# Tokens ordered by place in the chunk from the S5 inputs to the output projection of a hybrid S5 and FoX layer

## The chip, the cores and the metric

The kernel runs on one core of a Trainium2 chip. The metric is the device time of one execution in microseconds. A core has a matrix engine (PE in the profile), a vector engine (DVE), a scalar engine (ACT), a general engine (POOL) and a sync engine (SP), which here only issues DMAs. PE reads its operands from SBUF and writes into PSUM banks of 512 fp32 per partition; the other engines read those banks and empty them. [...]

## The reference, cut to what matters

A prompt of 2,048 tokens and a sample (decode) sequence of 64 tokens pass through one layer with 1,024 channels. Cut to its core:

```
shift, scale, gate = split(silu(c) @ w_ada + b_ada)
h    = rmsnorm(x) * (1 + scale) + shift
u, z_s, q, k, v, z_a, f_logit = split(h @ w_in)         # widths 512 x 6, then 8
y    = Re(C x_t) + D u,  x_t = abar * x_(t-1) + bbar u  # 32 groups of 16 channels, 64 complex states each
y    = gelu(y);  y = y * sigmoid(y @ w_glu + b_glu) * silu(z_s)
o    = softmax(q k^T / 8 + cumulative log-forget, causal) v * silu(z_a)   # 8 heads of 64
out  = x + gate * (concat(y, o) @ w_out)
return out, k, v, log-forget and last states, for prompt and sample
```

The decode sequence uses the same weights with given states and 512 cached keys and values per head.

## The kernel before, in words

The program is one Python builder. A list scheduler orders each engine's instructions ahead of time; in the last stage (the block `e.ordered()`) and on PE from the GLU on, the order is that of the code. All DMAs are issued by SP, one after another in SP's order, so a DMA whose data is late holds back those behind it. Products that need more than one fp32r pass are written as `mm3`: three matmuls with high and low halves (`whi`, `wlo`, and the two halves of `h`).

The stages follow each other: 

1. **Modulation and norm** (0 to about 144 us). `Ada` computes shift, scale and gate; `norm` loads x in tiles of 128 tokens, normalizes them and transposes them into `h` with channels on partitions. `h` has four groups g of 512 tokens; group 3 also holds the 64 decode tokens.
2. **In-projection and S5** (to about 750 us). `natural` makes u, k, v and q with tokens on PSUM partitions (`whi`, `wlo` stream as 256 columns, 24 matmuls per tile of 128 tokens; 264 columns where the eight forget logits ride along with u). `gates` makes the two z with channels on partitions, 512 tokens wide. u is done first; the other ten parts (k, k, v, v, q, q and four of z) are done for groups 2 and 3 and then again for 0 and 1, and beside each of them runs one of the 16 sets of the S5 (`s5_step`, two groups of 16 channels each). The S5 takes the sequence in 256 chunks of 8 tokens (and 8 decode chunks). Per set it needs u as a matrix `us` whose partitions are (token in the chunk, channel) and whose columns are the 264 chunks. Since `u_d` in DRAM is [token, channel], `load` fetches 128 chunks at a time with channels innermost (256-byte pieces) into `un`, DVE reorders a copy into `ug` (L920), PE transposes `ug`, and ACT copies PSUM into `us` (L943, L944). After the scan over the chunks (DVE, POOL and ACT), `outs` multiplies with `us` and `aa` (the scanned states) as stationary operands and the tables `tm` and `ca` as moving operands of 128 columns; 128 chunks land on the PSUM partitions, and the 8 decode chunks take matmuls of their own. ACT's gelu writes into `un`, and `ys_d` [token, channel] is stored from it.
3. **GLU** (750 to about 840 us). `Glu` reads `yn` from `ys_d` with tokens on partitions, PE transposes it (four per turn), ACT scales it into `y`, ACT and a second engine split it into `yh` and `yl`, and `mm` multiplies 256 tokens at a time with `wgh`, `wgl` into bank `glu`: nine token groups (one of them the 64 decode tokens) in two halves of the channels, 18 steps. POOL multiplies with z, the result goes to `ms_d` [channel, token]. Between the steps, the maxima for the attention's softmax run on PE and DVE.
4. **Attention** (840 to about 1,268 us). `Attn.run` goes through 20 tiles (four head pairs, five query tiles each). At a tile's end DVE multiplies the PSUM result by z, `sums` takes the reciprocal by Ln and Exp on ACT and multiplies on POOL, and the tile goes to `ma_d` [channel, token]. Meanwhile the generator `Out.weights` loads and splits w_out and combines operands for the last stage.
5. **Output projection** (to the end). `Out.run` multiplies `concat(ms, ma)` with w_out by Strassen's scheme in Winograd's form for seven pairs of 128-token tiles; pair 0 (`plain`) and the decode tokens are done directly. The products need the sums t1 to t4 of w_out's blocks (`operands`, done during parts 7 to 9 of the second half of stage 2, stored in DRAM, fetched again), and the loads `m` of `ms_d` and `ma_d` for the next pair.

In the profile, all matmuls bear the line of one helper (L144) and transposes that of another (L147), so groups are told apart by names.

## Time and profile before

| | us |
|---|---|
| runs | 1444.43, 1442.08, 1444.85 (median 1444.43) |
| the profiled execution | 1442.57, with a span of 1440.7 |
| PE busy | 1353.2 (94%) |
| DVE, ACT, POOL busy | 974.2 (68%), 593.1 (41%), 508.4 (35%) |
| TensorE clock granted, mean | 0.977 |
| DMA engines busy | 44.5% of 16 engines |

The span runs from the first to the last instruction; the profiled time has 1.9 us around it. A matmul group's "busy" adds up the durations of single matmuls that overlap in the engine's pipeline; what one costs is the distance between the starts of two that follow each other. An fp32 matmul leaves two records. "Idle before" names the wait that ended last in front of a group.

### The profile page before, as it was taken

Reading aid. Unit: us, or ns where it says so; the run is one execution under the profiler, and the core shown is the slowest. Engines: PE = TensorE matmul, PEld = TensorE weight load, DVE = VectorE, ACT = ScalarE, POOL = GpSimd, SP = SyncE. Lnnn points to the kernel's source line nnn. Section 1 sums busy time; section 2 is a strip of 40 time slices with the busy share of each in tenths; the row PEclk is TensorE's granted clock in tenths of the full one; section 3 lists DMA queues with packets and bytes.
Section 4 is the critical chain, followed back from the end, with each engine's and each line's share of the span. In section 5 each row is a group of like instructions: output and inputs, shape, how many; then the busy total and the mean of one; then the engine's idle time right before and its main releaser. Section 6 shows DMA issues by size and latency. Waiting matters only on the chain. (4 is left out here: it accounts for less than half of the span.)

```text
span 1440.7 us, 26308 instructions
## 1 busy us (share of the span) xinstructions
PE 1353.2 (94%) x9630; PEld 1065.7 (74%) x9630; DVE 974.2 (68%) x2455; ACT 593.1 (41%) x1252; POOL 508.4 (35%) x472
## 2 busy tenths in 40 slices
...
GB/s 339 282 288 158 124 65 87 98 83 92 112 96 149 280 75 142 65 116 140 218 331 294 176 146 128 40 54 132 41 76 52 75 60 81 133 235 217 161 161 88
DMA packets 210073, 205.01 MB, mean 142 GB/s; under 512 B 67575, under 2 KB 162515, under 8 KB 208920
## 3 DMA queue, kind: packets, MB, share of 16 engines
q1 hardware_dynamic: 209944, 203.33, 44.5%
...
## 5 line engine op out<-in xcount | busy, mean ns | idle before, releaser
L144 PE MATMUL low<-whi,h 128*128 128x256 f32 (+1 forms) x2112 | 406.1, 289 | 14.4 <-DVE ev L566 8.7
L144 PEld LDWEIGHTS low<-whi,h 128*128 128x128 f32 x2112 | 336.6, 192 | 24.8 <-issue 15.1
L144 PE MATMUL low<-wlo,h 128*128 128x256 f32 (+1 forms) x1088 | 307.5, 286 | 0.0
L1252 DVE CUSTOM_DVE_ANT_0 pb<-twin,cb 128x512 bf16<-128x512 f32 (+3 forms) x328 | 199.8, 609 | 68.4 <-PE twin L144 53.1
L144 PEld LDWEIGHTS low<-wlo,h 128*128 128x128 f32 x1088 | 209.0, 192 | 1.5 <-issue 1.2
L336 ACT ACTIVATE p<-twin 128x1024 f32<-128x1024 f32 (+3 forms) x180 | 149.4, 839 | 120.5 <-PE twin L144 113.5
L144 PE MATMUL low<-h,whi 128*128 128x512 f32 (+1 forms) x640 | 174.0, 357 | 0.0
L144 PE MATMUL bank<-p,vt 128*64 128x512 f32 (+3 forms) x704 | 143.5, 531 | 0.0
L144 PE MATMUL twin<-qs,ks 64*128 64x512 f32 (+3 forms) x1056 | 134.0, 359 | 0.0
L311 POOL TENSOR_TENSOR qss<-qss,mhalf 128x4 f32<-128x4 f32 (+1 forms) x68 | 77.2, 1136 | 139.9 <-DVE qss L310 117.3
L144 PEld LDWEIGHTS low<-h,whi 128*128 128x128 f32 x640 | 112.7, 188 | 17.7 <-issue 1.7
L305 DVE TENSOR_TENSOR wlo<-wst,whi 128x512 fp32r<-128x512 f32 (+1 forms) x96 | 67.3, 718 | 69.2 <-ACT whi L303 67.6
L144 PE MATMUL low<-h,wlo 128*128 128x512 f32 (+1 forms) x320 | 114.0, 356 | 0.0
L1329 DVE TENSOR_TENSOR acc<-acc,p 128x1024 f32<-128x1024 f32 (+4 forms) x90 | 87.8, 975 | 36.8 <-ACT p L336 35.1
L144 PEld LDWEIGHTS twin<-qs,ks 64*128 64x128 f32 x1056 | 94.8, 190 | 11.1
L144 PE MATMUL twin<-sm,kb 64*128 64x512 f32 (+3 forms) x360 | 78.0, 429 | 21.6 <-DVE pm L1252 12.5
L144 PEld LDWEIGHTS bank<-p,vt 128*64 128x64 f32 x704 | 45.4, 141 | 64.9 <-issue 56.8
L144 PEld LDWEIGHTS twin<-sm,kb 64*128 64x128 f32 x360 | 34.5, 187 | 63.8 <-DVE pm L1252 34.1
L303 ACT CAST whi<-wst 128x512 fp32r<-128x512 f32 (+1 forms) x96 | 57.2, 621 | 52.7 <-DMA wst<-in_w_in_dram 36.2
L195 POOL TENSOR_TENSOR x<-x,ot 128x512 f32<-128x512 f32 (+1 forms) x34 | 52.3, 1539 | 72.5 <-DVE ot L1633 66.1
L144 PE MATMUL twin<-ks,qs 64*128 64x512 f32 (+3 forms) x328 | 70.3, 432 | 4.0 <-ACT p L336 2.9
L1329 POOL TENSOR_TENSOR acc<-acc,p 128x1024 f32<-128x1024 f32 x22 | 52.4, 2383 | 42.9 <-ACT p L336 42.9
...
## 6 DMA issues: line engine op xcount, KB each, us to landing
...
```

The source lines that it names most:

```text
L144: return self.keep(self.pe.matmul(*a, **kw))
L195: PL.tensor_tensor(out, x, y, op=op)
L303: S.copy(hi, x)
L305: V.tensor_tensor(lo, x, hi, op=ALU.subtract)
L311: PL.tensor_tensor(out, out, bc(mhalf[:out.shape[0]], list(out.shape)), op=ALU.pow)
L336: i = S.activation(out, x, func, **kw)
L1252: V.tensor_tensor_reduce(b[:, :n], ps[:, h, :n], cb[:, h, :n], 1.0, NEG, ALU.add, ALU.max, accum_out=self.pm[:, t, h, pi:pi + 1])
L1329: (PL if j else V).tensor_tensor(y[:rows, :, c0:nq], x[:rows, :, c0:nq], p[:rows, :, :n], op=ALU.add)
```

## The change

The change keeps every tensor from u to the output projection's input in one order of tokens: by place t = 0 to 7 in the chunk, and inside a place by chunk (256 prompt chunks and 8 decode chunks, 264 in all).

- `u_d` and `ys_d` become [place, channel, chunk]; `z_d`, `ma_d`, `ms_d` become [channel, place, chunk]. A tile of 128 tokens is now half a place: `rows` picks every eighth row of x, y, k, v and q.
- `inputs` makes u with channels on partitions (256 or 320 tokens wide) instead of `natural`; the forget logits ride along with k, and `logf` moves from before `s5.setup` into the second half, behind part 1, with two switches of ACT's table; the log-forgets are written to DRAM and read back in token order.
- `load` is one DMA per group straight into `us`; the copy to `ug`, the transposes and ACT's copies go. `outs` has `tm` and `ca` stationary and streams `us` and `aa`, 264 columns, decode included; gelu writes `ys`, stored by one DMA per group.
- The GLU goes by place (8 places, two halves, 16 steps of 264 columns) and needs no transposes; its multiplication by z moves from POOL to DVE. 
- Attention's last multiplication on DVE reads PSUM with a stride and the one on POOL reads `w` with a stride of 8 elements.
- `operands` works on half blocks of 256 columns and is called in parts 4 to 8 of the second half. In the output projection, pair 0 is now place 0 and its ms half is multiplied first for all four blocks; its ma half and the load `m` of `ma_d` for pair 1 come right after the last attention tile; t4's eight fetches, which stood directly ahead of the next pair's loads `m` on SP, now follow pair 0's first half and stand behind that load; t3's last piece moves to the same place; the splits of w_out lag their loads by two.

Cut to its core ("..." marks what is left out):

```diff
-    u_d = dram.tile([NT, SW], F32, name="u_d")
+    u_d = dram.tile([TC, SW, CW], F32, name="u_d")
...
+    def rows(ap, i):
+        v = ap.rearrange("(c t) w -> t c w", t=TC)
+        return v[i // 2, P * (i % 2):P * (i % 2) + P] if i < 16 else v
...
-            nc.sync.dma_start(x[:r], e.x_p[t0:t0 + r] if s == 0 else e.x_s)
+            nc.sync.dma_start(x[:r], e.rows(e.x_s if s else e.x_p, i))
...
-                    nc.sync.dma_start(e.z_d[row:row + P, 512 * g + t0:512 * g + t0 + w], th[:, :w])
+                    nc.sync.dma_start(e.z_d[row:row + P, t:t + n, :NCH], th[:, :n * NCH].rearrange("p (t c) -> p t c", t=n))
...
+    def load(self, s):
+        us = self.us[s] = self.up.tile([P, GS, CW], F32, name="us", bufs=3)
+        for g in range(GS):
+            self.e.nc.sync.dma_start(us[:, g], self.group(self.e.u_d, GS * s + g))
...
-        for g in range(GS):
-            pt = self.pst.tile([P, 512], F32, tag="tr", name="tr")
-            for i in range(2):
-                PE.transpose(pt[:, P * i:P * i + P], ug[i][:, q0 + g], e.ident)
-            S.copy(us[:, g, :NCH], pt[:, :NCH])
-        S.copy(us[:, :, NCH:], self.ud[:, GS * s:GS * s + GS])
...
+        for g in range(GS):
+            py = self.ps.tile([P, CW], F32, tag="s5", name="sy")
+            PE.matmul(py, tm[:, g], us[:, g], start=True, stop=False)
+            PE.matmul(py, ca[:, g, 8:16].rearrange("p t q -> p (t q)"), aa[:, g], start=False, stop=True)
+            e.act(y[:, g], py, AF.Gelu_apprx_tanh)
+            nc.sync.dma_start(self.group(e.ys_d, GS * s + g), y[:, g])
...
+    def part(self, b):
+        if b < self.steps:
+            hl = self.yt[b] = [self.wk.tile([P, 2, CW], F32R, name="y" + i, bufs=4) for i in "hl"]
+            self.e.split(self.y[b], *hl)
...
-        e.V.scalar_tensor_tensor(xw, xw, 1.0, self.yt[b][0][:, :, :w], op0=ALU.add, op1=ALU.mult)
-        e.pmul(xw, xw, self.z[b][:, :, :w])
+        e.V.scalar_tensor_tensor(x, x, 1.0, self.y[b], op0=ALU.add, op1=ALU.mult)
+        e.V.scalar_tensor_tensor(x, x, 0.25, self.z[b], op0=ALU.mult, op1=ALU.mult)
...
-        e.pmul(w[:, :n], w[:, :n], tile.z[:, :n])
+        e.pmul(tile.z, w[:, :n].rearrange("p (c t) -> p t c", t=TC), tile.z)
...
+                if not half[0]:
+                    if part == 1:
+                        e.table("natural_log_exp_and_others", AF.Tanh, AF.Gelu_apprx_tanh)
+                        ip.logf(s5.ps)
+                        e.table("gelu_apprx_tanh_and_others", AF.Exp, AF.Ln, AF.Abs)
+                    for i in {4: (0,), 5: (1,), 6: (2, 3), 7: (4, 5), 8: (6, 7)}.get(part, ()):
+                        out.operands(*divmod(i, 2))
```

What this does to the order of the instructions shows at three places. The first is PE in an S5 set, among the matmuls of the in-projection (`bank` and `low` are PSUM banks). Before, transposes and the outputs of one bank:

```order
L147 MATMUL low_128<-ident_0_82,ug_192512_1_3165 128x128
L147 MATMUL low_128<-ident_0_82,ug_200704_1_3169 128x128
L147 MATMUL low_124<-ident_0_82,ug_192512_1_3165 128x128
L147 MATMUL low_124<-ident_0_82,ug_200704_1_3169 128x128
L144 MATMUL bank_77<-tm_1_1937,us_1_2832 128x128
L144 MATMUL bank_77<-ca_1_1923,aa_1_2833 128x128
L144 MATMUL bank_77<-tm_1_1937,us_1_2832 128x128
L144 MATMUL bank_77<-ca_1_1923,aa_1_2833 128x128
```

After, the outputs of a whole set (the first row belongs to the next set's scan):

```order
L145 MATMUL bank_81<-us_0_2396,bt_1_1842 128x264
L145 MATMUL low_144<-us_2_2730,tm_0_1823 128x264
L145 MATMUL low_144<-aa_0_2402,ca_0_1807 128x264
L145 MATMUL bank_77<-us_2_2730,tm_0_1823 128x264
L145 MATMUL bank_77<-aa_0_2402,ca_0_1807 128x264
```

Twelve matmuls per set of 128 columns (four of them for decode) become four of 264 columns, and the four transposes per set are gone.

The second place is PE between the last z of stage 2 and the first product of the GLU. Before:

```order
L144 MATMUL low_136<-h_16384_1_395,wlo_0_211 128x512
L147 MATMUL bank_77<-ident_0_82,yn_0_8142 128x128 x4
L147 MATMUL bank_81<-ident_0_82,yn_0_8142 128x128 x4
L147 MATMUL bank_77<-ident_0_82,yn_1_8146 128x128 x4
L144 MATMUL glu_8123<-yh_0_8157,wgh_0_8140 128x256
```

After:

```order
L145 MATMUL low_140<-h_53248_1_394,whi_0_209 128x512
L145 MATMUL low_140<-h_16384_1_393,wlo_0_210 128x512
L145 MATMUL glu_7905<-yh_0_7942,wgh_0_7922 128x264
L145 MATMUL glu_7905<-yl_0_7943,wgh_0_7922 128x264
L145 MATMUL glu_7905<-yh_0_7942,wgl_0_7923 128x264
```

The GLU's first instruction no longer is a transposition of `yn` but a product of the split `yh`.

The third place is DVE in `s5.setup` (`un`, `uo`, `wre`, `wim`, `btt` are its tables). Before:

```order
L841 TENSOR_TENSOR btt_174848_0_1877<-pre_113536_0_1537,b1_124288_0_1848 128x256
L666 TENSOR_TENSOR uo7_165568_0_1638<-wim_161984_0_1572 128x32
L666 TENSOR_TENSOR un7_165440_0_1637<-un7_165440_0_1637,uo7_165568_0_1638 128x32
L672 TENSOR_SCALAR un7_165440_0_1637<-un7_165440_0_1637 128x32
L666 TENSOR_TENSOR wre_160832_0_1571<-wre_160832_0_1571,un7_165440_0_1637 128x32
L666 TENSOR_TENSOR wim_161984_0_1572<-wim_161984_0_1572,un7_165440_0_1637 128x32
L666 TENSOR_TENSOR wre_160832_0_1571<-wre_160832_0_1571 128x32
L666 TENSOR_TENSOR cn2_158528_1_1754<-tb1_117888_0_1568,wre_160832_0_1571 128x64
```

After (`t2`, `b..` and `pl` belong to `operands`):

```order
L880 TENSOR_TENSOR btt_174848_0_1798<-btt_174848_0_1798,lin_175872_0_1799 128x256
L704 TENSOR_TENSOR uo7_165568_0_1559<-wim_161984_0_1493 128x32
L1512 TENSOR_TENSOR t2_141824_0_6829<-b11_140800_0_6824,b00_137728_0_6821 128x256
L312 TENSOR_TENSOR pl_147968_0_6835<-b11_140800_0_6824,ph_142848_0_6834 128x256
L878 TENSOR_TENSOR lin_175872_0_1799<-pim_114688_0_1459,c2_130432_0_1784 128x288
L704 TENSOR_TENSOR un7_165440_0_1558<-un7_165440_0_1558,uo7_165568_0_1559 128x32
L312 TENSOR_TENSOR pl_148992_1_6841<-b01_138752_0_6822,ph_143872_1_6840 128x256
L710 TENSOR_SCALAR un7_165440_0_1558<-un7_165440_0_1558 128x32
L312 TENSOR_TENSOR pl_150016_2_6847<-t2_141824_0_6829,ph_144896_2_6846 128x256
L704 TENSOR_TENSOR wre_160832_0_1492<-wre_160832_0_1492,un7_165440_0_1558 128x32
```

Though the code calls `operands` in parts 4 to 8 of the second half, the scheduler puts most of it here, since nothing holds it back: 31 of its 48 DVE instructions stand ahead of the first scan of the S5, the others within the first four sets; before, all of them stood behind the last set. Its loads of w_out and its 64 stores of half blocks move with them on SP. The small operations of `logf` (19 on L620 and two on L621, among others) that stood in this stretch are gone from it.

380 lines of the change are left out of this document (173 added, 207 removed).

## The prediction

> **What bounds the kernel now.** I read the page's busy times first, then the busy times by stretch, then PE's waits, and last the timeline where the change acts.
>
> ```profile
> span 1440.7 us, 26308 instructions
> PE 1353.2 (94%) x9630; PEld 1065.7 (74%) x9630; DVE 974.2 (68%) x2455; ACT 593.1 (41%) x1252; POOL 508.4 (35%) x472
> ```
>
> The columns of the next view are the stretch, its length, the busy time of PE, of its weight loads, of DVE, ACT and POOL, then the TensorE clock granted, the share of the DMA engines and GB/s.
>
> ```profile
> 144.00:216.00 72.00, 62.48 (x495) 61.47 (x494) 65.49 (x319) 18.12 (x48) 29.97 (x38) 0.96 0.36 95
> 216.00:750.00 534.00, 518.75 (x3697) 474.18 (x3696) 366.31 (x880) 216.03 (x603) 183.69 (x211) 0.99 0.45 137
> 750.00:840.00 90.00, 79.58 (x656) 72.98 (x657) 44.85 (x132) 42.61 (x94) 49.35 (x43) 0.92 0.76 241
> ```
>
> PE sets the end nearly everywhere. In the S5 stretch (216 to 750) it is busy for 518.75 of 534 us, and DVE has a third of its time to spare: a matmul that goes there shortens the run by its own time, as long as the next one's data is ready. Two stretches are different. In the setup of the S5 (144 to 216) DVE is busy for 65.49 of 72 us, more than PE. At the start of the GLU PE stands still:
>
> ```profile
> PE bank L147 <- DMA z_d<-th: 7.7, 1, 7.7
> 749.62 0.40 PE L144 MATMUL low<-h,wlo 128*128 128x512 f32 x1
> 757.70 1.08 PE L147 MATMUL bank<-ident,yn 128*128 128x128 f32 x4 [7.68 <-DMA z_d<-th]
> 752.51 0.37 SPq L1452 DMA_DIRECT2D yn<-ys_d  x1
> 752.00:766.00 14.00, 7.38 (x31) 6.40 (x32) 1.24 (x2) 3.93 (x7) 8.84 (x10) 0.52 1.02 362
> 768.00:772.00 4.00, 4.00 (x36) 4.00 (x35) 1.20 (x2) 2.64 (x7) 2.62 (x3) 1.00 1.01 296
> ```
>
> The first `yn` is issued only at 752.51, behind stores of z in SP's queue, and the DMA engines are full (1.02). After the gap the clock stands at 0.52 until 766. So the stop costs 7.7 us, and the work that runs at half clock between 757.7 and 766, some 9 us of it mostly busy, costs about 4.5 us more: 12.2 in all.
>
> **The change part by part.** Prices are distances between starts, since matmuls overlap.
>
> *The S5's outputs.*
>
> ```profile
> 247.46 0.38 PE L144 MATMUL bank<-ca,aa 128*128 128x128 f32 x2
> 249.22 0.38 PE L144 MATMUL low<-whi,h 128*128 128x256 f32 x1
> 229.05 0.61 PE L144 MATMUL bank<-us,bt 128*128 128x264 f32 x2
> 229.73 0.28 PE L144 MATMUL low<-wlo,h 128*128 128x256 f32 x1
> ```
>
> Between the first two rows stand sixteen records of outputs, the decode ones among them, in 1.76 us: 0.11 each, 0.22 for a matmul of two records. Twelve per set in 16 sets are 192 x 0.22 = 42.2 us. The new matmul of 264 columns has a twin in the trace, `us,bt`: between the last two rows lie one of it and two matmuls with `h`, at 0.12 each (below), which leaves 0.44; four per set, 64 x 0.45 = 29. **Minus 13.**
>
> *Transposes of u.*
>
> ```profile
> L147 PE MATMUL low<-ident,ug 128*128 128x128 f32 x64 | 11.3, 276 | 0.8 <-DVE kd L868 0.8
> L147 PE MATMUL bank<-ident,yn 128*128 128x128 f32 x64 | 11.3, 309 | 7.7 <-DMA z_d<-th 7.7
> 230.32 0.60 PE L147 MATMUL low<-ident,ug 128*128 128x128 f32 x4
> 230.88 0.28 PE L144 MATMUL low<-wlo,h 128*128 128x256 f32 x1
> 785.00 0.28 PE L144 MATMUL glu<-yh,wgh 128*128 128x256 f32 x1
> 785.12 0.28 PE L144 MATMUL glu<-yl,wgh 128*128 128x256 f32 x1
> ```
>
> Four transposes and one matmul with `h` take 0.56 us (230.32 to 230.88), so one transpose is 0.11: 64 of them, **minus 7**. u itself with channels on partitions streams 313,344 columns per pass with the two z of group 3 where 315,392 were: 2,048 fewer at 0.12 per 256, **minus 1**. The copies to `ug` and `us` on DVE and ACT lie beside PE, and I count them only in the setup below.
>
> *The GLU's own work.* 68 transposes of `yn` at 0.11 go (7.5). Of its products, 384 of 256 columns at 0.12 (785.00 to 785.12) and 48 of the 64 decode tokens, which I take at 0.11 since the transpose of 128 columns has that too, become 384 of 264 columns at 0.124: 51.4 against 47.6. Two steps fewer means that seven DVE operations of the maxima move into the attention; of some 0.7 us each there I let 1.5 show. **Minus 10.** The second multiplication on DVE is hidden: DVE is busy for 45 of 90 us here.
>
> *The GLU's start.* Four `y` are loaded ahead and split directly, and nothing on PE waits for a transposition. What then is late is the bank: the first GLU product now takes banks that the last z has to leave, a tanh on ACT and a product on DVE (0.68 us for the latter):
>
> ```profile
> L590 DVE SCALAR_TENSOR_TENSOR th<-th,low 128x512 f32<-128x512 f32 x24 | 16.3, 680 | 21.4 <-ACT th L336 21.3
> L303 ACT CAST whi<-wst 128x512 fp32r<-128x512 f32 (+1 forms) x96 | 57.2, 621 | 52.7 <-DMA wst<-in_w_in_dram 36.2
> ```
>
> [...] **Minus 10.4**; at worst nothing, if `y` comes as late as `yn` did; at best minus 12.2.
>
> The stores of z now move pieces of 1 KB, and 32 bytes for decode, and u, the S5's outputs and the attention's tiles move as pieces of 1,056 or 256 bytes. The nearest row is the old `un<-u_d`, all in pieces of 256 bytes: it was issued at 272.29 and its 256 KB went through in the stretch 273 to 276.
>
> ```profile
> 272.29 0.58 SPq L915 DMA_DIRECT2D un<-u_d  x1
> 274.00:275.00 1.00, 1.00 (x11) 0.91 (x8) 1.00 (x4) 0.72 (x5) 0.14 (x1) 1.00 1.06 268
> 840.00:1268.00 428.00, 404.24 (x3186) 222.65 (x3184) 307.06 (x780) 204.25 (x285) 155.85 (x88) 0.97 0.27 83
> ```
>
> [...]
>
> *The output projection.*
>
> ```profile
> 1296.02 0.38 SPq L1554 DMA_DIRECT2D oh<-t  x1
> 1299.84 0.38 SPq L1645 DMA_DIRECT2D m<-ms_d  x1
> 1307.99 1.29 POOL L195 TENSOR_TENSOR ms<-m,m 128x512 f32<-128x512 f32 x1 [6.95 <-DMA m<-ma_d]
> 1314.29 0.50 PE L144 MATMUL last<-oh,mha 128*128 128x512 f32 x1 [2.08 <-DVE ot L1701]
> 1316.00:1320.00 4.00, 4.00 (x13) 3.18 (x12) 4.00 (x4) 0.62 (x1) 2.35 (x2) 0.62 0.17 66
> ```
>
> Eight fetches of t4 stand ahead of `m` on SP, POOL waits for `m` for 6.95 us, and PE then for 2.08 us and 1.7 more at the lower clock. With `m` of `ma_d` issued right after the last tile and t4 behind it, this goes: **minus 3.8**. The same place gets a new dependency, pair 0's ma half behind the last tile's store; pair 0's ms half and the decode tokens cover it. POOL's multiplication there reads with a stride of 32 bytes:
>
> ```profile
> L195 POOL TENSOR_TENSOR w<-w,z 128x512 f32<-128x512 f32 x16 | 20.5, 1283 | 20.8 <-DMA ht<-t 16.4 <-ACT w L336 2.8 <-DVE mq L1256 1.5
> ```
>
> [...]
>
> *The setup of the S5.* This is the part that speaks against the change. On DVE, 31 of the 48 operations of `operands` now stand in front of the S5's first scan. Before, they ran at 690 to 744 us, where DVE had slack:
>
> ```profile
> 690.00:744.00 54.00, 54.00 (x249) 43.68 (x248) 31.25 (x43) 20.49 (x37) 11.96 (x8) 1.00 0.77 267
> 144.00:234.00 90.00, 80.48 (x641) 78.62 (x640) 80.60 (x365) 25.29 (x70) 41.05 (x55) 0.96 0.34 91
> L305 DVE TENSOR_TENSOR pl<-b,ph 128x512 fp32r<-128x512 f32 x12 | 10.9, 925 | 2.9 <-ACT ph L303 1.5 <-DMA t<-pl 1.3
> L620 DVE TENSOR_TENSOR off<-off,bank 128x8 f32<-128x8 f32 x15 | 2.2, 149 | 0.0
> L920 DVE COPY ug<-un 128x512 f32<-128x512 f32 x16 | 9.0, 563 | 8.5 <-DMA un<-u_d 8.5
> ```
>
> A half-width operation is about 0.45 us, half of 0.925: 31 of them bring 14 us. Out of the same stretch go `logf` (19 x 0.15 = 2.9, and about as much for its larger operations and gaps) and three copies to `ug` (1.7). DVE, busy for 80.60 of 90 us there, gets about 6.5 us more than before, and its free 9.4 are gaps between dependent operations rather than slack. PE has fewer of its own matmuls to pass the time with. I take **plus 5** (bounds 0, if the gaps take it, and 15, if it shows in full, with POOL slowing DVE and a window of half clock).
>
> *Later costs.* `logf` in the second half still has its chain, and two switches of ACT's table: **plus 2** (0 to 4). The sets' outputs now wait for both `us` and `aa` with fewer matmuls between; I let **plus 3** of the 20 us saved there come back as waits (0 to 10).
>
> *Loads of x.* In the first 36 us the DMA engines are full. x now comes in rows of 4 KB with a pitch of 32 KB. Nothing in the trace shows such a pitch; the rows are as long as before, so I take nothing, with 8 us as the upper bound (a fifth of the time that ends with this row):
>
> ```profile
> 18.00:36.00 18.00, 16.22 (x96) 7.45 (x92) 3.49 (x12) 3.93 (x8) 0.00 (x0) 1.00 1.05 382
> ```
>
> Sum: -13 -7 -1 -10 -10.4 -3.8 +5 +2 +3 = -35.2, against the profiled execution's own 1442.6: **1407 us**. That execution lies 1.9 us under the median of the three runs, within their spread, and I leave that out.
>
> **Rivals.** *More gain.* [...] Over the span the clock averages 0.977, that is 33 us of lost clock, of which only some 6 are in my sum. If the setup costs nothing and the gaps in the S5 (about 15 us idle) shrink with the DVE copies, 1407 - 5 - 5 - 10 = 1387. Against it: most of those gaps wait for DVE, which has no less to do there.
>
> *Half the gain.* The S5's sets are paced by DVE wherever `operands` or a setup runs, so PE's 20 us there only half show (+7 beside the 3 counted), and `y` arrives late for the GLU (+10): 1424. For it speaks that DVE is full at 144 to 234; against it the 0.69 of DVE over the S5 stretch.
>
> *Slower.* DVE becomes the bound from the setup to the fourth set. Each of the 48 operations of `operands`, at half width with POOL beside it, takes the 0.925 of the full-width row above, 44 us, and all of it shows on PE, and the waits halve the clock for a third of that again, as they do at 144 to 216 (9.5 idle, 0.04 x 72 = 2.9 lost): 44 x 1.3 = 57, in place of the 5 and the 3: 1407 + 49 = 1456. It decides above 35 + 8 = 43 us of waiting.
>
> *The change doesn't do what it says:* the order of the instructions shows that the transposes and the small matmuls go, so only their time could stay, and that is the half-gain case.
>
> **How the numbers follow.** My forecast (1394 to 1418) has 0.5, more gain 0.17, half the gain 0.24, slower 0.06, and 0.03 for something near no change. The likeliest is 1407. The range, reaching into the cases on both sides, is 1382 to 1434. Faster by more than 0.2% (what a measurement of this kernel can tell from no change) 0.91, within it 0.03, slower 0.06.
>
> **What would show it.** Right: no transposes of u or y in the groups; four output matmuls per set 0.45 us apart; PE's wait at the GLU's start under 3 us with a clock above 0.9 in the 14 us after; no wait of `ms<-m,m` on POOL near 7 us. In the setup, PE busy for less of the stretch up to the first scan than before, with waits on DVE. Wrong: a PE wait over 5 us at the GLU's start, waits on DVE of more than 25 us in the S5 stretch, or a first stretch of 144 us that has become longer.

## The result: slower, with less work on PE

The changed kernel takes 1477.46 us (median of four runs, 1473.75 to 1478.42), the kernel before 1443.26 on the same chip: a ratio of 1.0233 (95% interval 1.0209 to 1.0256). I had forecast 1407, with 1382 to 1434 as the range. The size and the direction are both wrong.

The head of the page of the changed kernel:

```profile
span 1474.5 us, 25463 instructions
PE 1339.8 (91%) x9160; PEld 1045.4 (71%) x9160; DVE 982.2 (67%) x2472; ACT 567.6 (38%) x1164; POOL 500.4 (34%) x460
```

PE has 13 us less to do even by its busy time, in which work at the lower clock counts for longer (a product of 264 columns in the changed kernel takes 0.22 us from its start to the next one's at half clock, at 188.38, and 0.12 at full clock, at 191.56), and DVE only 8 us more. (Busy time here, of an engine or of a group, is the time in which at least one of its instructions runs; instructions that overlap are not added up.) So the loss is not work but time in which PE stands still or runs slowly. To see where, I cut both spans at the same events: the last transposition of x, the first tile of k that is normalized, the first product of a z on DVE, the last tile of q, the last product of a z, the last GLU output and the last tile of the attention. Four of these stages, first before, then after (the columns are the stretch, its length, busy PE, weight loads, DVE, ACT and POOL, the clock granted, the share of the DMA engines and GB/s):

```profile
181.00:372.00 191.00, 180.48 (x1420) 171.80 (x1421) 154.37 (x450) 75.87 (x236) 91.10 (x107) 0.97 0.31 87
372.00:657.00 285.00, 275.88 (x2068) 257.62 (x2066) 198.59 (x489) 114.82 (x327) 93.42 (x115) 0.99 0.43 131
755.00:838.00 83.00, 78.67 (x648) 72.49 (x648) 42.06 (x126) 38.58 (x88) 43.68 (x40) 0.93 0.75 234
838.00:1268.00 430.00, 405.13 (x3191) 223.14 (x3189) 308.92 (x785) 206.13 (x288) 156.66 (x88) 0.97 0.27 83
```

```profile
188.00:422.00 234.00, 198.08 (x1390) 182.49 (x1391) 207.47 (x582) 93.83 (x291) 125.33 (x150) 0.93 0.43 131
422.00:692.00 270.00, 257.68 (x1830) 240.96 (x1829) 161.84 (x433) 91.02 (x235) 82.09 (x92) 0.98 0.43 131
780.00:854.00 74.00, 64.66 (x519) 58.98 (x519) 53.00 (x123) 28.90 (x59) 19.55 (x15) 0.95 0.79 231
854.00:1298.00 444.00, 412.10 (x3205) 227.06 (x3204) 317.37 (x805) 206.00 (x289) 158.72 (x87) 0.95 0.30 77
```

From the same view in steps of one microsecond I split each stage of PE into three parts that add up to its length: idle (1 minus busy), lost to the clock (busy times 1 minus the granted clock), and the rest, which is its work at full speed:

| stage | before: length, idle, clock, work | after: length, idle, clock, work |
|---|---|---|
| norm, u | 135, 21.9, 1.6, 111.5 | 138, 26.3, 5.8, 105.8 |
| to the first k | 46, 5.1, 0, 40.9 | 50, 7.8, 0, 42.2 |
| to the first z | 191, 10.5, 5.0, 175.5 | 234, 35.9, 12.0, 186.0 |
| to the last q | 285, 9.1, 3.1, 272.8 | 270, 12.3, 3.0, 254.7 |
| to the last z | 98, 5.0, 0, 93.0 | 88, 1.1, 0, 86.9 |
| GLU | 83, 4.3, 3.7, 74.9 | 74, 9.3, 2.4, 62.3 |
| attention | 430, 24.9, 13.2, 391.9 | 444, 31.9, 19.5, 392.6 |
| output projection | 172.7, 6.7, 1.7, 164.3 | 176.5, 10.1, 2.3, 164.1 |
| all | 1440.7, 87.6, 28.3, 1324.9 | 1474.5, 134.8, 45.0, 1294.8 |

The work fell by 30.1 us. This measure is good to some 6 us only: e9 and e10 below have the same matmuls and come out at 1293.7 and 1287.5. The terms of my sum that are work on PE (outputs 13, transposes of u 7, u itself 1, GLU 10) make 31. So that half of the sum was right, and 47.2 us of idleness and 16.7 us of clock ate it twice over. Most of the loss is the stage from the first k to the first z: 43 us longer, with DVE's busy time up from 154.4 to 207.5 us. It gets part of that back in the stages behind (work has moved forward), and the attention loses 14 more.

The waits of PE in that stage, before and after (us in total, times, longest):

```profile
PE low L144 <- DVE ev L566: 3.7, 2, 3.3
PE low L144 <- DVE ca L842: 3.6, 2, 2.1
PE low L144 <- DVE wre L666: 3.0, 1, 3.0
```

```profile
PE low L145 <- DVE ev L597: 14.3, 9, 4.9
PE low L145 <- DVE qss L317: 8.2, 2, 4.8
PE low L148 <- DVE btt L880: 3.9, 1, 3.9
PE bank L145 <- DVE aa L982: 2.7, 1, 2.7
```

`ev` and `qss` are the normalization of k: I read these rows so that a product on PE cannot start because an earlier tile, waiting for DVE, still holds its bank. The stage falls into two pieces, each with its neighbour before:

```profile
182.00:307.00 125.00, 117.10 (x949) 113.00 (x948) 98.53 (x304) 49.67 (x158) 56.67 (x71) 0.97 0.30 86
307.00:372.00 65.00, 62.49 (x469) 57.89 (x468) 54.84 (x143) 26.20 (x80) 34.43 (x37) 0.97 0.31 90
```

```profile
189.00:334.00 145.00, 122.49 (x908) 116.42 (x907) 119.87 (x341) 54.87 (x169) 71.41 (x90) 0.93 0.50 152
334.00:422.00 88.00, 74.61 (x483) 65.06 (x482) 86.59 (x235) 38.95 (x123) 53.82 (x60) 0.94 0.32 96
430.00:515.00 85.00, 84.13 (x525) 76.57 (x524) 28.71 (x52) 21.20 (x45) 6.25 (x7) 1.00 0.52 163
```

In the first piece (k of the first half with the S5's setup) DVE has 21 us more than before. In the second (q) it is full, 86.59 of 88 us, and right behind that, at 430 to 515, it is two thirds idle. The starts of the first scan of each of the S5's sixteen sets, taken from the timeline and rounded, show what has moved:

```
before  234 243 273 303 324 345 393 426 456 481 498 523 548 601 620 656   (first z: 372)
after   242 262 279 303 339 353 373 388 409 423 521 533 578 595 645 673   (first z: 422)
```

Before, six sets begin ahead of the first z. After, nine do and a tenth follows at once, and then none for 98 us.

### The profile page after: what moved, and what is told of

The parts are those of the page before. It is cut to its first block, busy times and chain, and to the rows that moved or that the text cites. A ratio compares the mean times of both kernels' runs of the same rounds, so it can differ in the third digit from the quotient of the medians.

```text
span 1474.5 us, 25463 instructions
## 1 busy us (share of the span) xinstructions
PE 1339.8 (91%) x9160; PEld 1045.4 (71%) x9160; DVE 982.2 (67%) x2472; ACT 567.6 (38%) x1164; POOL 500.4 (34%) x460
## 4 chain that ended last, share of the span: by engine, by line
PE 63%; DVE 18%; DMA 8%; issue 4%; ACT 3%; POOL 3%; SPq 1%; ACTq 0%; DVEq 0%; POOLq 0%
PE low L145 25%; PE twin L145 13%; PE bank L145 12%; PE last L145 8%; PE glu L145 2%; PE bank L148 2%; DVE pb L1244 2%; DMA x<-in_x_prompt_dram 1%; DMA ost<-in_w_out_dram 1%; DMA wst<-in_w_in_dram 1%; DVE wlo L312 1%; DVE ev L598 1%; POOL qss L318 1%; DVE z L966 1%; DVE ev L597 1%
## 5 line engine op out<-in xcount | busy, mean ns | idle before, releaser
L145 PE MATMUL low<-whi,h 128*128 128x256 f32 (+1 forms) x1584 | 311.3, 293 | 32.3 <-DVE ev L597 18.2
L145 PEld LDWEIGHTS low<-whi,h 128*128 128x128 f32 x1584 | 257.7, 196 | 40.6 <-issue 15.0
L145 PE MATMUL low<-h,whi 128*128 128x256 f32 (+2 forms) x1152 | 274.8, 330 | 6.0 <-ACT th L550 4.8
L145 PE MATMUL low<-wlo,h 128*128 128x256 f32 (+1 forms) x816 | 233.9, 289 | 0.4 <-DVE wlo L312 0.3
L145 PEld LDWEIGHTS low<-h,whi 128*128 128x128 f32 x1152 | 196.2, 192 | 26.1 <-ACT th L550 5.9
L145 PE MATMUL low<-h,wlo 128*128 128x256 f32 (+2 forms) x576 | 187.3, 328 | 0.0
L145 PEld LDWEIGHTS low<-wlo,h 128*128 128x128 f32 x816 | 159.3, 195 | 2.1 <-DVE wlo L312 1.0
L145 PEld LDWEIGHTS low<-h,wlo 128*128 128x128 f32 x576 | 110.5, 192 | 9.4 <-issue 1.0
L318 POOL TENSOR_TENSOR qss<-qss,mhalf 128x4 f32<-128x4 f32 (+1 forms) x68 | 89.7, 1321 | 61.5 <-DVE qss L317 51.3
L145 PE MATMUL twin<-sm,kb 64*128 64x512 f32 (+3 forms) x360 | 78.3, 431 | 24.9 <-DVE pm L1244 13.6
L620 DVE SCALAR_TENSOR_TENSOR th<-th,low 128x512 f32<-128x512 f32 (+2 forms) x40 | 23.6, 591 | 95.7 <-ACT th L343 95.4
```

Of the source, the lines that this page charges most:

```text
L145: return self.keep(self.pe.matmul(*a, **kw))
L318: PL.tensor_tensor(out, out, bc(mhalf[:out.shape[0]], list(out.shape)), op=ALU.pow)
L620: V.scalar_tensor_tensor(th[:, :w], th[:, :w], 1.0, pm[:, :w], op0=ALU.add, op1=ALU.mult)
```

## The experiments

The theory at the start had two causes, the hoisted `operands` and the sets that run ahead, with the shared pacer DVE. The rivals were the smaller queue effects (stores of the attention, loads of `m`) and a kernel that DVE paces wherever the sets stand. The stage lengths of the runs, cut as above, that the text below refers to (each from one execution, to about a microsecond; that of e3 lies 5 us above the median of its run and that of e11 4 above, that of e17 6 below):

| run | norm | k | to z | to q | last z | GLU | attention | out |
|---|---|---|---|---|---|---|---|---|
| before | 135 | 46 | 191 | 285 | 98 | 83 | 430 | 173 |
| after | 138 | 50 | 234 | 270 | 88 | 74 | 444 | 176 |
| e1 | 140 | 44 | 223 | 280 | 85 | 87 | 443 | 177 |
| e2 | 137 | 49 | 206 | 292 | 84 | 74 | 448 | 176 |
| e3 | 137 | 45 | 194 | 293 | 86 | 87 | 446 | 177 |
| e4 | 139 | 49 | 234 | 273 | 87 | 74 | 442 | 176 |
| e5 | 138 | 44 | 223 | 288 | 87 | 74 | 444 | 176 |
| e6 | 138 | 44 | 193 | 317 | 84 | 76 | 442 | 177 |
| e7 | 139 | 49 | 234 | 272 | 87 | 74 | 441 | 180 |
| e8 | 126 | 51 | 195 | 318 | 85 | 75 | 440 | 176 |
| e9 | 139 | 44 | 194 | 294 | 84 | 75 | 442 | 178 |
| e10 | 137 | 45 | 188 | 287 | 84 | 75 | 447 | 178 |
| e11 | 128 | 51 | 194 | 291 | 97 | 75 | 444 | 173 |
| e12 | 127 | 51 | 198 | 293 | 97 | 78 | 439 | 173 |
| e13 | 128 | 51 | 194 | 298 | 84 | 76 | 442 | 172 |
| e14 | 126 | 51 | 194 | 298 | 84 | 76 | 444 | 173 |
| e15 | 127 | 51 | 194 | 297 | 85 | 75 | 441 | 172 |
| e16 | 127 | 50 | 196 | 300 | 84 | 83 | 429 | 172 |
| e17 | 128 | 50 | 194 | 295 | 85 | 75 | 427 | 183 |
| e18 | 126 | 51 | 195 | 294 | 88 | 76 | 427 | 183 |

All kernels start from the changed one. Ratios are to the kernel before on the same chip, with 95% intervals.

**Run e1: `operands` out of the setup.** Its loads wait for the last store of the part where the code has them, so the scheduler can't hoist them.

```
-            e.nc.sync.dma_start(b, self.block(i // 2, i % 2, k)[:, ns])
+            d = e.nc.sync.dma_start(b, self.block(i // 2, i % 2, k)[:, ns])
+            e.tc.add_manual_dep(d.ins, e.mark.ins.name, e.nosync)
```

> The changed kernel with one edit: each load of operands is ordered behind the last store of the projection's part at which the code calls it, so that operands runs in parts 4 to 8 of the second half and not in the setup. Theory 1 (operands takes DVE from the setup and the first sets): between DVE's first reduction of k (182 us) and the first reduction of q (333 us) the changed kernel loses 22.5 us idle and 7.3 us of clock, against 7.9 and 3.4 before; most of the 18.5 comes back, and the run is 1455 to 1462. Rival (the S5's sets stand too close together and DVE is full there with or without operands): the stretch stays long, the gain is under 8 us, 1470 or more.

Measured 1478.2, 1.0214 (1.0188 to 1.0239): no gain. But the stage did change. The two pieces from the first k to the first z in this run:

```profile
184.00:316.00 132.00, 118.82 (x898) 111.62 (x898) 97.34 (x295) 46.46 (x140) 60.19 (x75) 0.95 0.28 85
316.00:407.00 91.00, 74.05 (x484) 64.56 (x483) 90.27 (x236) 39.57 (x123) 56.29 (x63) 0.94 0.30 90
```

The first piece falls from 145 to 132 us, DVE's busy time there to that of the kernel before, and the k stage from 50 to 44. The second piece stays. The first z comes 15 us earlier, at 407, and the GLU then gives 13 us back (below, e3). So `operands` in the setup costs what the k stage and the first piece show, 6 and 13 us, but late in the second half, near where it was before, it no longer fits either. The edit moves the loads and stores of `operands` along with its work on DVE, so e1 alone does not tell the two apart; of PE's waits in this stage of the changed kernel, the four rows above are for DVE (29.1 us), and 1.6 us are for a DMA.

**Run e2: the sets paced.** The first products of a set on PE wait for the last matmul of the part of the projection before the one beside which the code has the set.

```
-            PE.matmul(pv, bt[:, g], us[:, g], start=True, stop=True)
+            m = PE.matmul(pv, bt[:, g], us[:, g], start=True, stop=True)
+            if PE.mark:
+                PE.tc.add_manual_dep(m.ins, PE.mark, PE.dep)
...
+                mark = e.PE.latest
                 if done[0] <= NSET:
...
+                e.PE.mark = mark
```

> The changed kernel with one edit: the first matmul of each S5 set is ordered on PE behind the end of the projection part before, so that sets 6 to 9 can't run ahead of the gates as they do now (ten sets between 242 and 429 us, then none until 521). Theory 2 (sets that run ahead fill DVE between 333 and 418 us): the 13.4 us idle and 4.3 us of clock there fall to the 2.5 and 1.6 of before, and the run is 1460 to 1467. Rival (theory 1 alone): no set's start before 333 us changes, less than 5 us is gained.

Measured 1467.43, 1.0142 (1.0120 to 1.0163): 10 us gained. The two pieces:

```profile
186.00:331.00 145.00, 122.81 (x905) 117.34 (x906) 120.92 (x353) 54.26 (x167) 75.96 (x92) 0.92 0.50 156
331.00:392.00 61.00, 57.21 (x410) 53.09 (x409) 52.84 (x149) 23.95 (x72) 30.78 (x34) 0.97 0.34 101
```

This is the mirror image of e1: the first piece stays at 145 with `operands` in it, the second falls from 88 to 61 with DVE at 52.84. The two causes are separate, and each has its own piece.

**Run e3: both edits.**

> Both edits of the two runs before together. If the two causes are separate, the gains add: 1477 - 18 - 14 = 1445 or so, and PE's waits in the S5 stretch come back to about 15 us. If they are one (DVE is short in the first half, whatever fills it), the two together gain not much more than the better one.

Measured 1461.52, 1.0108 (1.0082 to 1.0134), and not the 1445 of two gains that add. The row from the first k to the first z:

```profile
182.00:376.00 194.00, 178.14 (x1319) 167.57 (x1318) 156.78 (x453) 72.13 (x218) 94.44 (x114) 0.96 0.30 90
```

It takes 194 us with DVE at 156.8; the kernel before has 191 and 154.4. So 40 of the 43 us are explained. The GLU, however, takes 87 us, and this is the longest single wait of PE in the run:

```profile
PE glu L147 <- ACT wgh L312: 13.4, 1, 13.4
```

ACT's split of the GLU's weights waits 11.65 us for their load, which SP issues at 760.50, behind the last stores of `operands` (757.48). Their buffers lie in the same part of SBUF. Where `operands` stand earlier (e2, e5) there is no such wait and the GLU takes 74 us.

**Run e4: the attention's store on the old side.** Ln writes its tile by place, so that POOL reads without a stride.

```
-        e.act(w[:, :n], pt[:, :n], AF.Ln, scale=2.0)
+        wv = w[:, :n].rearrange("p (t c) -> p t c", t=TC)
+        e.act(wv, pt[:, :n].rearrange("p (c t) -> p t c", t=TC), AF.Ln, scale=2.0)
-        e.pmul(tile.z, w[:, :n].rearrange("p (c t) -> p t c", t=TC), tile.z)
+        e.pmul(wv, wv, tile.z)
```

> The changed kernel with one edit in the attention: ACT's Ln writes its result already in the order by place, so POOL multiplies w by z in one order and writes to w, and the store of ma_d reads w, not the tile of z. Theory 3 (the next tile's load of z on SP waits for the store out of the same buffer, 47.6 us in 18 waits, and the loads of w_out behind it come late to ACT and so to PE): the waits of z's load for ma_d's store go, the attention (444 us, 31.9 idle and 19.5 clock) comes back to some 432, the run to 1465. POOL's multiplication falls from 1.62 to 1.28 us. Rival (the loads of w_out are late because their buffers come free late, or the attention loses by the maxima moved into it): under 4 us.

Measured 1474.57, 1.0188 (1.0164 to 1.0213). The attention is 2 us shorter. The rows of POOL's product by tile names (minimum, median, maximum ns), before and after; in this run its mean is 1094 over all twenty:

```profile
L195 POOL TENSOR_TENSOR w<-w,z x20: 320/1280/1297, 860.9 to 1274.6; 128x512 f32<-128x512 f32 x16, 128x64 f32<-128x64 f32 x4
```

```profile
L196 POOL TENSOR_TENSOR z<-w,z x20: 343/1622/1664, 879.2 to 1302.7; 128x512 f32<-128x512 f32 x16, 128x64 f32<-128x64 f32 x4
```

The stride costs 0.34 us per tile on an engine that is busy for a third of the span. It is not where 14 us of the attention went.

**Run e5: `operands` in the first half's gates.** With e1's edit, two half blocks follow each of parts 6 to 9 of the first half.

```
-                    for i in {4: (0,), 5: (1,), 6: (2, 3), 7: (4, 5), 8: (6, 7)}.get(part, ()):
-                        out.operands(*divmod(i, 2))
+                if half[0] and part > 5:
+                    for n in range(2):
+                        out.operands(part - 6, n)
```

> The changed kernel with operands ordered behind the stores of the four gate parts of the first half, two half blocks each, where DVE has little to do. In the run with operands in parts 4 to 8 of the second half, the stretch of the setup was shorter by 19 us (6 and 13), but the GLU longer by 13, with the first products waiting for the GLU's weights. Theory 1 in its new form (operands costs what it displaces: DVE in the setup, or SP's queue, DMA engines and the GLU's buffers at 690 to 760 us): the setup's 19 us come back as there, and the GLU stays at 74 us: 1460. Rival (the DVE time moved only shows up elsewhere): 1470 or more.

Measured 1477.79, 1.0248 (1.0218 to 1.0277). The GLU is free of the weights' wait (74 us), but the stage to the last q is 8 us longer than in e1, with PE idle for 24.5 us of it instead of 15.4.

**Run e6: that, with the sets paced.**

> The same, with the S5's sets paced as in the second run. Both at once gave 1461.5 with the GLU at 87 us. Theory: that less the 13 of the GLU, 1447 to 1450, with the last gates at 755 us as before the change. Rival (the gates' parts now hold S5 sets and operands, and DVE fills there): the stretch from the first gates to the last reduction of k gets longer by more than 5 us than its 177.

Measured 1473.66, 1.0230 (1.0192 to 1.0268). The first z is as early as before (375), and the stage behind it takes 317 us instead of 285. PE is idle there for 31.2 us and loses 15.2 to the clock. The sets now stand in this stretch, and `operands`, put there in a lump, cost more than in the setup.

**Run e7: `m` ahead of the decode loads.** The decode tokens' loads wait for the load of `m` in SP's order.

```
+            d = e.nc.sync.dma_start(m[:, k].rearrange("p (t c) -> p t c", t=TC), (e.ms_d, e.ma_d)[j][P * k:P * k + P, :, NCH:])
+            e.tc.add_manual_dep(d.ins, self.loaded.ins.name, e.nosync)
```

> The changed kernel with one edit: the decode tokens' loads of ms_d (four DMAs of 32-byte pieces), which stand ahead of the 512 KB load m that ACT's cast of mha needs, are ordered behind it. Theory 4 (those pieces make m late by 5 us, ACT's cast in front of the last exponentials waits 7.5 us for m and PE 4.7 us behind it, then a half-clock window): ACT's wait falls under 3 us, the attention shortens by 4 to 8 us, the run is 1469 to 1473. Rival (m is late because its buffer is free late): nothing changes, 1477.

Measured 1474.86, 1.0224 (1.0190 to 1.0259). Three us less in the attention, four more behind it: nothing.

**Run e8: all repairs so far.** e3's pacing, e5's place for `operands`, e4, e7, and four buffers instead of two for u:

```
-                    u = self.ev.tile([P, 512], F32, tag="th", name="th")
+                    u = self.ev.tile([P, 512], F32, tag="th", name="th") if w > 256 else self.ev.tile(
+                        [P, 256], F32, tag="ev", name="ev", bufs=4)
```

> The changed kernel with all edits so far (operands in the first half's gate parts, sets paced, Ln's result by place, m ahead of the decode loads) and one more: u leaves PSUM through four buffers instead of two, since ACT's copies of u wait 7.5 us for the stores of u before 140 us where they waited 2.1 in the kernel before. The gains add up if they are separate: 1448 - 3 - 5 - 5 = 1435, faster than the kernel before (1443 to 1447). If the attention's gaps only move, 1443 or more.

Measured 1466.95, 1.0168 (1.0140 to 1.0196). The norm stage falls from 138 to 126 us, 9 below the kernel before. In the change ACT's copies of u wait for their buffers' stores, before and after (ACT's waits in that stage):

```profile
ACT ev L555 <- DMA u_d<-ev: 2.1, 1, 2.1
```

```profile
ACT th L550 <- DMA u_d<-th: 7.5, 5, 2.7
```

But the next stage is 51 us instead of 44 to 46. I read this as the setup, which DVE paces, not ending earlier by as much. Of the 12 us, 4 arrive at the first z.

**Run e9: few `operands`.** e3 with one quarter of the products (what is left out stands in the expectation).

```
-                    for i in {4: (0,), 5: (1,), 6: (2, 3), 7: (4, 5), 8: (6, 7)}.get(part, ()):
+                    for i in {6: (0, 1)}.get(part, ()):
```

> The changed kernel with the S5's sets paced as in the second run, and with operands left out for three of the four rows of blocks (the two half blocks of row 0 stay, in part 6 of the second half; the products fetch row 0 four times, so their values are not the reference's). It shows what operands costs wherever it stands: the second run has it in the setup, 1467. Theory 1: the setup up to the first reduction of q comes to 182 and 311 us as in the third run, the GLU stays at 74 us, and the run is 1445 to 1450. Since PE has some 30 us less to do than before the change, 1445 would also say that something else holds the first half. Rival: above 1457.

Measured 1451.8, 1.0066 (1.0042 to 1.0091). Against e2, where all of them stand in the setup, that is 15.6 us; against e3, 9.7, which the GLU accounts for (75 us instead of 87). Even so it is slower than the kernel before, although PE has some 30 us less to do. The stage to the first z is 194 us, not below.

**Run e10: less work on DVE.** e9 without the product with the gains of q and k on DVE.

```
-                    V.tensor_tensor(tv, tv, gw[:r].unsqueeze(1).to_broadcast([r, 4, HD]), op=ALU.mult)
```

> The run before, with one thing more left out: DVE's multiplication of k and q by their norm gains (68 operations of 0.42 us, 28 us in all, half of them in the first half). PE's instructions are the same. Theory 5 (from the setup to the last S5 set it is DVE's chain that sets the pace, so that matmuls taken off PE leave waits and no time): the first half's k and q parts shorten by 8 to 14 us and the run by 15 to 25, PE's waits falling by as much. Rival (PE's own work sets the pace): less than 6 us.

Measured 1441.26, 0.9990 (0.9971 to 1.0009): 10.5 us less than e9. DVE's busy time fell by 24 us in the whole run (963.9 to 940.1). The rows from the first k to the first z, of e9 and of this run:

```profile
183.00:377.00 194.00, 177.10 (x1321) 166.05 (x1321) 157.80 (x453) 71.90 (x215) 94.59 (x115) 0.96 0.30 90
182.00:370.00 188.00, 175.10 (x1324) 165.79 (x1324) 143.95 (x420) 72.71 (x221) 92.61 (x114) 0.97 0.31 93
```

PE's matmuls are the same. So the time in this stretch follows DVE's work at some 0.43 of its price (6 us of 13.9; 10.5 of 23.8 in the run), although DVE is busy for only four fifths of it. The theory had asked for 15 to 25 us and the rival for less than 6: DVE sets a part of the pace, and not all of it.

**Run e11: `operands` late, loads repaired.** e8's other edits, `operands` in parts 5 to 7 of the second half, and the eight fetches of t4 behind `load(2)`.

```
+                    for i in {5: (0, 1), 6: (2, 3, 4), 7: (5, 6, 7)}.get(part, ()):
-        for k in range(4):
-            self.fetch("t4", k, self.b["b12", k])
...
         self.load(2)
+        for k in range(4):
+            self.fetch("t4", k, self.b["b12", k])
```

> A repaired version: the changed kernel with operands in parts 5 to 7 of the second half (part 5 two half blocks, 6 and 7 three each, so that they end before the GLU's weights need their buffers), paced sets, Ln's result by place, m ahead of the decode loads, four buffers for u, and t4's fetches behind the loads of pair 2 on SP. Against the third run (1461.5): 12 us less in the GLU, 4 less in the output projection if t4 in front of m is what POOL waits for (10.2 us), 5 less in the attention: 1440. If the GLU's weights or y still come late, 1450.

Measured 1451.36, 1.0054 (1.0036 to 1.0073). The output projection falls from 176 to 173 us; the stretch of the z, 97 us, now bears `operands`.

**Run e12: the gains' product on POOL.**

```
-                    V.tensor_tensor(tv, tv, gw[:r].unsqueeze(1).to_broadcast([r, 4, HD]), op=ALU.mult)
+                    e.pmul(tv, tv, gw[:r].unsqueeze(1).to_broadcast([r, 4, HD]))
```

> The run before, with the multiplication of k and q by the norm gains on POOL instead of DVE; nothing is left out. Theory 5: 28 us less on DVE at the price of some 50 on POOL, which is busy for 36% of that stretch: 8 to 15 us less than the run before, 1425 to 1432, faster than the kernel before the change. Rival (POOL's slower multiplication lengthens the way from PSUM to the next matmul): no gain.

Measured 1457.28, 1.0103 (1.0079 to 1.0127): 6 us worse than e11. POOL's product for k (mean 917 ns for each of 34) against DVE's mean of 439 ns in e11:

```profile
L198 POOL TENSOR_TENSOR ev<-ev,kg 128x256 f32<-128x256 f32 (+1 forms) x34 | 31.2, 917 | 20.4 <-ACT ev L596 5.6 <-DVE ev L600 5.0 <-issue 4.8
```

I read this as the tile's chain having become longer by more than DVE's relief was worth; the run does not separate that from POOL's other work being delayed.

**Run e13: `operands` spread over parts 3 to 7.** Otherwise e11.

```
-                    for i in {5: (0, 1), 6: (2, 3, 4), 7: (5, 6, 7)}.get(part, ()):
+                    for i in {3: (0, 1), 4: (2,), 5: (3,), 6: (4, 5), 7: (6, 7)}.get(part, ()):
```

> The eleventh run (1451.4) with operands spread over parts 3 to 7 of the second half: two half blocks in part 3 (v, where DVE has little to do), one each in 4 and 5, two each in 6 and 7. There each half block took some 10 us from its loads to the next one's (one buffer per block), the last ended at 748 us, and the stretch from the last q to the last z was 97 us with 8.7 idle, where the ninth run without operands took 84. Theory: that stretch comes to 85 to 88 and the run to 1441 to 1444. Rival (operands in the q parts costs DVE there what it saves): 1449 or more.

Measured 1445.73, 0.9999 (0.9980 to 1.0018). The level of the kernel before is back. Its norm, GLU and last z are 28 us shorter than before; the stages to the first k (+5), the first z (+3) and the last q (+13) and the attention (+12) take that away. Split as above, PE has 33.0 us less work than in the kernel before (1291.9), 15.1 more idle (102.7) and 22.1 more lost to the clock (50.4).

**Run e14: no lag in splitting w_out.** The lag of two tiles between load and split in the attention is taken away.

> The same, with each block of w_out split right after its own load in the code, as in the kernel before the change, and not two loads later. Theory 6 (the lag is what the attention loses: ACT waits 27 us for blocks of w_out in ten waits where it waited 21.6, and PE behind it for the exponentials, then a half clock): the attention, 440 to 444 us in all repaired runs against 430 before the change, comes to 434 or less, the run gains 6 to 10. Rival (the waits come from SP's order or from chance in where the half-clock windows fall): under 3 us.

Measured 1445.91, 1.0010 (0.9988 to 1.0031): no effect.

**Run e15: pair 0's splits after the attention.** They move from the generator in the attention to the start of the last stage. In this run and the next the load of pair 1 overwrites pair 0's ms half before that split, so that pair 0's product is computed with pair 1's data. Instructions and bytes are the same, but that load waits for less than it has to; e17 has the right order.

```
-        for name in ("a11", "a21"):
-            self.split(0, name)
-            yield
...
         self.residual(2)
+        self.split(0, "a11", "a21")
```

> The thirteenth run (1445.7) with one edit: the splits of pair 0's ms half, whose cast on ACT waits 5.8 us for its load m in front of the attention's last exponentials, are moved behind the attention, ahead of the decode products. Theory 7 (at the attention's end PE waits behind ACT for a load, and each such gap of 1.5 to 4 us costs half-clock time on top: 5.1 us of clock lost at +402 us where it was 3.4 before the change): the gaps from +380 us on (3.8 us idle and 5.1 of clock) go or shrink, the attention comes from 442 to 436, the run to 1438 to 1441, at or under the kernel before. If the products at the start of the output projection now wait for these splits instead, that stretch (172 us) gets longer by as much, 1445.

Measured 1441.43, 0.9996 (0.9975 to 1.0017). The attention is one microsecond shorter than in e13: the splits are not what stretches it.

**Run e16: the maxima back in the GLU.** Each step of the GLU takes two calls of the attention's maxima along (products on PE, reductions on DVE, seven DVE operations by my count in four of them). With 16 steps instead of 18 there is room for four calls fewer. This edit makes it 36 again. Many calls find nothing to do: by the traces, of the 336 reductions on DVE 44 start before the GLU's last product ends in the kernel before, 36 in the changed one and in e15, 40 in this run.

```
-            for _ in range(MXU):
+            for _ in range(MXU + (b % 4 == 1)):
```

> The run before with one more edit: four more slots for the attention's maxima in the GLU (36, as before the change, where the changed kernel has 32), so that DVE has fewer left in the attention's first 25 us. There PE waits 3.2 and 1.3 us for maxima on DVE (1.1, 0.7 and 1.6 before the change), and 6.8 and 1.7 us of clock are lost. If the deferred maxima are the cause: 2 to 4 us less in the attention, with up to 2 more in the GLU. If the order inside the attention is: nothing.

Measured 1442.45, 0.9986 (0.9965 to 1.0006). GLU and attention of e13 and of this run:

```profile
755.00:831.00 76.00, 66.52 (x519) 60.95 (x519) 52.69 (x123) 29.68 (x60) 19.88 (x17) 0.93 0.77 225
831.00:1273.00 442.00, 414.68 (x3202) 228.01 (x3201) 315.84 (x802) 205.65 (x289) 154.24 (x87) 0.95 0.30 77
```

```profile
757.00:840.00 83.00, 68.45 (x520) 62.46 (x521) 55.01 (x129) 29.13 (x60) 19.77 (x16) 0.92 0.70 206
840.00:1269.00 429.00, 404.30 (x3199) 222.41 (x3201) 314.92 (x796) 206.09 (x289) 157.30 (x87) 0.97 0.30 80
```

So four reductions more in the GLU, half of what had moved, bring the attention from the 441 of e15 to 429 us, the 430 of the kernel before, and the GLU from 75 to 83. e17 and e18, which keep the edit, have 427. So this edit takes back what the attention had lost. How it does so is open: PE's work there is the same (393.3 and 392.8 us), its idle time falls by 5 us and the clock's loss by 6, and only 2 of these 11 us lie in its first 30 us. And the run as a whole gained nothing over e15 (1441.43).

**Run e17: more buffers for the GLU's output.** e16 with three buffers for `gx` and five for `yt`, and pair 1's load moved behind pair 0's split.

```
-        x = self.wk.tile([P, 2, CW], F32, tag="gx", name="gx")
+        x = self.wk.tile([P, 2, CW], F32, tag="gx", name="gx", bufs=3)
...
```

> The sixteenth run with its loads put right (pair 1's load m follows the splits of pair 0, so the output is the reference's again), and with three buffers instead of two for the GLU's result (and five instead of six for its input). In all versions since the change PE waits once for 4.3 to 5.4 us in the GLU's second step, because ACT's tanh has no free buffer: the store of the first result is held up on SP behind four loads of v. Theory: that wait and the half clock behind it go, the GLU comes from 83 us to 76 or 77, and the run to 1434 to 1437, faster than the kernel before. Rival (the step after it meets the same held-up stores): 1441.

Measured 1445.14, 1.0014 (0.9994 to 1.0034). The GLU is at 75 and the attention at 427, both good, and the last stage takes 183 us instead of 172 (13.3 us idle and 4.6 of clock, where e16 has 7.1 and none). That the moved load of pair 1 does this is argued (PE waits there 4.8 us for `ot`, 2.8 for `mhs` and 1.0 for `mls`, against 2.2 for `ot` alone in e16), not tried by itself.

**Run e18: the second gate product on POOL.** The factor 0.25 goes to ACT in front, so that POOL can multiply with z as in the kernel before.

```
-        e.V.scalar_tensor_tensor(x, x, 0.25, self.z[b], op0=ALU.mult, op1=ALU.mult)
+        e.pmul(x, x, self.z[b])
...
```

> The run before with the GLU's multiplication by z back on POOL (ACT scales y by 0.25 for it, as before the change). DVE has 55 us of work in the GLU's 83, 11 of them by this multiplication that the change moved there. Theory (GLU with the maxima is paced by DVE's chain): PE's waits for maxima there (5.9 us) fall, 2 to 6 us less, 1430 to 1434. Rival (DVE has time there and PE waits only for single operations): within 2 us of the run before, or slower by POOL's longer multiplication (1.28 for 0.71 us).

Measured 1444.9, 1.0010 (0.9990 to 1.0029): as e17.

No version beats the kernel before beyond its interval. The repairs bring 1.0233 down to 1.00 (e13, e17 and e18 among those that compute the whole layer), and there the freed time of PE comes back as idle time and lost clock.

## Why the prediction was wrong, step by step

**What bounds the kernel.** The step that failed first is the sentence that in the S5 stretch a removed matmul shortens the run by its own time "as long as the next one's data is ready". It rested on PE being busy for 518.75 of 534 us. The condition does not hold: the tiles of k and q, the setup and the sets give PE's banks back by way of ACT and DVE (in the traces of the two kernels these two read banks, in the kernel before `ev<-low` on ACT 128 times and `ev<-low,qss` on DVE 64 times, and no row of POOL has a bank as its input), and DVE's work sets a part of their pace. That PE was full because its work was about as long as that chain is my reading. e3 fits it: with both causes of the loss undone, PE has 4.8 us less work to the first z than the kernel before (170.7 against 175.5), and takes 194 us instead of 191. e10 shows the other side: with the same matmuls on PE and 14 us less on DVE than e9 it takes 188 us instead of 194. DVE's busy share (0.69 over the stretch) hid this; I take it that a chain through ACT, DVE and POOL can be full while each engine has gaps.

**PE's own terms** (-13, -7, -1, -10) were right as work: -30.1 measured against -31. From each start to the next on PE, the outputs take 43.8 us in the kernel before and 30.1 in the changed one, where the sum had 42.2 and 29. They were wrong as time, except behind the S5: the last z and the GLU are 19 us shorter, with 18.7 us less work.

**The setup, +5 (bounds 0 to 15).** Mis-sized. The 32 products at half width had the right price:

```profile
L312 DVE TENSOR_TENSOR pl<-b,ph x24: 407/412/1355, 169.0 to 273.5; 128x256 fp32r<-128x256 f32 x24
```

I took 0.45 us, the median is 0.41. What was wrong was to set them against the leaving operations and gaps. Between the first k and q DVE's busy time rose by 21 us and the piece by 20 (145 against 125); e1, without them, has 132. e9 against e2 gives 15.6 us for three quarters of them left out and the rest moved, in the whole run; e1's two stages give 6 and 13. By either, all of them cost 16 to 21 us here, over the upper bound of 15, which allowed for one stretch at half clock; the clock alone took 7.3 us in that piece instead of 3.4. That POOL slows DVE, which the bound also allowed for, shows in the traces at times: in the kernel before the products of full width took 0.69 us with POOL idle (722.29) and 1.74 with an operation of POOL beside them (716.68); of the 32 in the changed kernel three took 1.20 to 1.35 us with POOL beside them (229.46, 249.85, 252.25), and another, with POOL beside it too, 0.43 (196.64).

**The S5's waits, +3 (0 to 10).** The step looked for waits between `us`, `aa` and the outputs. What happened is another thing: the sets were no longer held back and ran ahead of the gates. In e2, holding them back took 27 us out of the second piece and 10 out of the run. What had held them in the kernel before I can only argue: `un` had its own buffers and load per group, with a copy and transposes behind it, and all that is gone. I had read their removal as a saving only.

**The GLU's start, -10.4.** The gap in front of the GLU I had misread. The first `yn` did not wait behind stores of z. The GLU's weights come in through the same buffers, and SP waited for POOL's split of them: POOL's two products end at 752.48 and 754.78, and the first two `yn` go out at 752.51 and 754.81. SP's wait in the kernel before:

```profile
SPq L1452 <- POOL wgl L195: 3.5, 2, 2.2
```

In the change the inputs have buffers of their own, and the wait at the first matmul became 1.41 us. No run shows the 1.8 us of waiting that the term leaves of its 12.2, nor that a wait of that length always leaves the clock alone; what was measured is these 1.41 us, with the clock at 1.00 from 780 to 792. But nothing of the 10.4 arrived: over the last z and the GLU together PE's idle time and lost clock are 13.0 us before and 12.8 after. What was late next is ACT's buffer. First PE's first matmul, then ACT's stop behind it and SP's queue, and last PE's waits for `gx`:

```profile
780.35 0.39 PE L145 MATMUL glu<-yh,wgh 128*128 128x264 f32 x1 [1.41 <-DVE th L620]
```

```profile
793.73 0.85 ACT L343 ACTIVATE gx<-glu,hbg 128x264 f32<-128x264 f32 x2 [3.49 <-DMA ms_d<-gx]
```

```profile
781.35 6.06 SPq L1186 DMA_DIRECT2D vt<-out_dram  x4
787.52 1.02 SPq L1446 DMA_DIRECT2D yt<-ys_d  x1
788.65 1.05 SPq L1476 DMA_DIRECT2D ms_d<-gx  x1
```

```profile
PE glu L145 <- ACT gx L343: 6.1, 2, 4.3
```

A store of the first `gx` stands on SP behind four loads of v that hold the queue for 6.06 us; ACT has no buffer of `gx` free until that store has landed, and PE waits 4.3 us for ACT. With more buffers for `gx` (e17) this wait falls to 1.3 us in all. I had asked what is late after `yn`, and answered with the bank, which was right for the first matmul; I did not follow the first output through SP's queue. That the clock stayed full behind the first wait was luck: in the kernel before, a wait of 1.46 us has a stretch at half clock behind it, and another of 1.46 us has none (last section).

**The maxima, 1.5.** Mis-sized, if one goes by the stages: e16 against e15 is 12 us less in the attention and 8 more in the GLU, 4 net for half of the reductions that moved, where I had let 1.5 show for all. The medians of the two runs (1442.45 and 1441.43) do not show these 4 us.

**The output projection, -3.8.** Failed on a reading of the order. I wrote that `m` is issued right after the last tile with t4 behind it. That is so for pair 1, whose difference on POOL waits 1.95 us. The wait of 6.95 us was for the load of pair 2, and for that one t4 still stands ahead on SP in the changed kernel (with a load of x and three stores between):

```profile
1329.64 1.10 SPq L1524 DMA_DIRECT2D olb<-t  x1
1333.03 0.62 SPq L1627 DMA_DIRECT2D m<-ms_d  x1
1333.74 0.98 SPq L1627 DMA_DIRECT2D m<-ma_d  x1
```

```profile
1312.06 1.29 POOL L196 TENSOR_TENSOR ms<-m,m 128x512 f32<-128x512 f32 x1 [1.95 <-DMA ht<-t]
1341.14 1.27 POOL L196 TENSOR_TENSOR ms<-m,m 128x512 f32<-128x512 f32 x1 [10.16 <-DMA m<-ma_d]
```

The wait grew from 6.95 to 10.16 us, and PE's one wait in this stage from 2.1 to 5.6. e11 does what I had read into the change: t4 stands behind that load. It has the stage at 173 instead of 176, and this wait:

```profile
1320.63 1.29 POOL L198 TENSOR_TENSOR ms<-m,m 128x512 f32<-128x512 f32 x1 [7.08 <-DMA m<-ma_d]
```

That is the 7 us of the kernel before, PE's wait is 2.5 us, and the stage as long as in the kernel before. So the fetches ahead of `m` were not what made those 7 us, and even with t4 behind `m` the term comes to about nothing. In e11 the load of `ma_d` goes out at 1313.65, behind three stores, and POOL starts 7 us later.

**Costed at nothing.** The loads of x with a pitch: right (383 GB/s at 18 to 36 us, against 382 before). POOL's strided product has no term in the sum: it took 1.62 us instead of 1.28, and without the stride (e4) the attention is 2 us shorter. The pieces of 256 bytes have none either: over the attention the DMA engines are at 0.30 with 77 GB/s, where they were at 0.27 with 83. u's copies with two buffers instead of four were not in the sum: +3 us in the norm stage instead of the gain of 9 that e8 shows.

**The rivals.** "Half the gain" had the mechanism, DVE as the pacer of the sets wherever `operands` or a setup runs, and priced it at 7 us beside the 3 counted; its other half, a late `y`, did not come. "Slower" named the right place and gave 1456 to it with a chance of 0.06; its price per operation was too high, and it knew nothing of the sets that bunch. Of the signs I had listed for being wrong, waits on DVE over 25 us in the S5 stretch came true (the four groups quoted above are 29.1 us in that one stage), and so did a longer first stretch (138 us instead of 135, as cut above); no wait over 5 us stood at the GLU's start. Of the signs for being right, the transposes are gone, the new outputs are 0.44 us apart, and the GLU's start has its short wait with the clock at 0.93 in the 14 us after; these came true while the time did not: they tell of work and of inputs, and none of them of the buffers behind. The chance of 0.91 for faster came from counting only what leaves PE.
